# Two edits to a hybrid trunk kernel: where the first chunk products stand, and which engine multiplies row block 6 of the stick-breaking weights

## The chip, the cores and the metric

The kernel runs on one core of one Trainium2 chip. Its engines work side by side, each through its own list of instructions in a fixed order: TensorE (PE in the profile, PEld for its weight loads), VectorE (DVE), ScalarE (ACT), GpSimd (POOL) and SyncE (SP), which here mostly issues transfers. An instruction waits until what it needs is there, and everything behind it on the same engine waits with it. The metric is the time of one execution on the device in microseconds (us).

## The reference, cut to what matters

One layer on a sequence of 1024 tokens, model width 1024, float32. Three groups of heads mix the tokens, then comes a SwiGLU feed-forward part of hidden width 2816.

```python
h = rms_norm(x, attn_norm_g) @ w_in
r, k, v, wd, ad, gd = split(token_shift(h[..., :RW_COLS], mu))      # RWKV-7, 8 heads of 64
c_q, c_kv, k_rope, sb_q, sb_k, sb_v = split(h[..., RW_COLS:])       # latent, stick-breaking
# RWKV-7, per head and token:
S = S * w_t + (S @ a_t) b_t^T + v_t k_t^T        # a = -kk, b = kk * sigmoid(..), kk = normalised k
y_t = S @ r_t                                     # then group norm, bonus, gate
# stick-breaking, 4 heads of 64, s < t:
A[t, s] = sigmoid(z_ts) * prod_{s<j<t} (1 - sigmoid(z_tj));  y = A @ v
# latent attention, 4 heads: softmax over chunks up to the query's own
x = x + concat(y_rw, y_mla, y_sb) @ w_o
hn = rms_norm(x); x = x + (silu(hn @ w_gate) * (hn @ w_up)) @ w_down
```

## The kernel before, in words

A float32 product is made of three products of rounded parts (`mm3`, lines 207 to 209: high times high, high times low, low times high), so a projection of 128 columns against 512 tokens is 24 products. The weights of each are loaded by SP into `wr`, rounded into `wh` by ACT (line 185), and their rest `wl` comes from GpSimd (line 93, the helper that records every two-input operation).

**RWKV heads in pairs.** The eight heads go as four pairs `pr`, the 1024 tokens as two halves `hf`. `rw_block(pr, which)` projects k, r or v of one pair: two halves of 24 products each, then `shifted` (lines 288 to 298) takes them out of PSUM: ACT scales a half into SBUF (line 292), DVE adds the neighbour token's part (line 297). `between` is a tuple of functions that are called between the two halves and whose work is so written between them. `s1` makes the decays (u, ua, the scan `cs`, `Pe`, `iP`); `s2` makes the norm (ss, rs), kkn, and the factors `AR`, `BK` and `BD` of the chunk products, and `av`; `s3` makes the chunk products g (32 small products, masked by DVE into `gs`), and vt, bo and bkt, transposed copies that go out by DMA as `vs`, `av` and `bks`. `BD` has one buffer; PSUM has eight banks of 512 columns, shared in turn by projections, g, vt, bo, bkt, ss, u and ua.

**What sets the order.** The functions are written pair by pair so that the `s3` of one half stands between projections of the next. The program's builder then deals the instructions out to the engines by a cost model of its own, and each engine keeps that order. So an edit at one place can move rows at others.

**Stick-breaking.** For each of four heads and each row block i of 128 queries, `sb_weights` makes the scores z, two sigmoids on ACT (`st` and `w`), a running product `C` over the keys from the right (a scan on DVE, line 997, spans of up to 512 columns), and then w times C (line 93). `SB_POOL` (line 1110) lists the row blocks whose product w times C goes to GpSimd; the others go to DVE. The first entry of C is filled by GpSimd (line 985). `st`, `w` and `C` share a ring of five buffers. After it `av_tasks` transposes w on TensorE (wt, line 926), splits it (`wth` on ACT, `wtl` on DVE) and multiplies by v. In this stage the steps of the RWKV state chain (y, u, s) and the latent attention's rows are interleaved.

Of the kernel before, what the change touches and what calls it, by code (L numbers as in the profile page):

```python
# [59 lines left out]
def trunk_kernel(ctx: ExitStack, tc: tile.TileContext, a: dict, out: bass.AP):  # L60
# [17 lines left out]
    def bank(name, tag="b"):  # L78
        return psum["pool"].tile([P, HALF], F32, tag=tag, bufs=psum["tags"][tag], name=name)
# [12 lines left out]
    def tt(eng, o, x, y, op):  # L92
        eng.tensor_tensor(o, x, y, op=op)  # L93
# [21 lines left out]
    def vcol(r):  # L115
        return vec[:, r : r + 1]
# [109 lines left out]
    def inproj_cols(c0, name, between=()):  # L226

        if name in begun:
            return begun.pop(name)
        w = in_weights(c0, name)  # L230
        os_ = [in_half(w, 0, name)]
        for f in between:
            f()
        return os_ + [in_half(w, 1, name)]
# [53 lines left out]
    def shifted(dst, os_, cb):  # L288

        for hf in range(2):  # L290
            o, d_ = os_[hf], dst[hf]
            nc.scalar.activation(d_, o, AF.Copy, scale=omu[:, cb : cb + 1])
            if hf == 0:
                nc.vector.tensor_scalar_mul(car[:, cb : cb + 1], o[:, HALF - 1 : HALF], vcol(R_MU + cb))
            else:
                tt(nc.vector, d_[:, 0:1], d_[:, 0:1], car[:, cb : cb + 1], ALU.add)
            nc.vector.scalar_tensor_tensor(d_[:, 1:HALF], o[:, 0 : HALF - 1], vcol(R_MU + cb), d_[:, 1:HALF],
                                           op0=ALU.mult, op1=ALU.add)
# [50 lines left out]
    with tc.tile_pool(name="qa", bufs=1, reuse_waits="tile") as qa:  # L349
# [37 lines left out]
        def h2(name, tag, bufs=1):  # L387
            return qa.tile([P, HALF], F32, tag=tag, bufs=bufs, name=name)

        def ch8(ap):  # L390
            return ap.rearrange("p (c t) -> p c t", t=L)
# [24 lines left out]
        def rw_block(pr, which, between=()):  # L416

            t_ = [h2(f"{'KRV'[which]}{pr}{hf}", "KRV"[which], 3) for hf in range(2)]
            cb = (4 + pr, pr, 8 + pr)[which]
            shifted(t_, inproj_cols(cb * P, f"{'krv'[which]}{pr}", between), cb)  # L420
            KRV[pr][which] = t_
# [36 lines left out]
        def s2(pr, hf):  # L458
            n = f"{pr}_{hf}"
            sq, av, Pe, iP = tmp[n]  # L460
            k_, r_ = KRV[pr][0][hf], KRV[pr][1][hf]
            oss = bank(f"ss{n}")
            nc.tensor.matmul(oss, onesblk, sq, start=True, stop=True)
            rs_ = h2(f"rs{n}", "s1", 2)
            nc.scalar.activation(rs_, oss, AF.Ln, bias=EPS12)
            nc.scalar.activation(rs_, rs_, AF.Exp, scale=-0.5)
            kkn = h2(f"kkn{n}", "kkn")
            nc.vector.scalar_tensor_tensor(kkn, k_, vcol(R_KK + pr), rs_, op0=ALU.mult, op1=ALU.mult)
            AR = qa.tile([P, 8, 2, L], F32, tag="AR", bufs=2, name=f"AR{n}")
            BK = qa.tile([P, 8, 2, L], F32, tag="BK", bufs=2, name=f"BK{n}")  # L470
            nc.vector.scalar_tensor_tensor(AR[:, :, 0, :], ch8(kkn), -1.0, Pe[:, :, 0:64], op0=ALU.mult, op1=ALU.mult)
            tt(nc.gpsimd, AR[:, :, 1, :], ch8(r_), Pe[:, :, 1:65], ALU.mult)
            tt(nc.vector, kkn, kkn, av, ALU.mult)
            tt(nc.vector, BK[:, :, 0, :], ch8(kkn), ch8(iP), ALU.mult)
            nc.vector.tensor_scalar(av, av, vcol(R_KA + pr), oka[:, pr : pr + 1], op0=ALU.mult, op1=ALU.add)
            tt(nc.vector, av, av, k_, ALU.mult)
            tt(nc.vector, BK[:, :, 1, :], ch8(av), ch8(iP), ALU.mult)
            nc.vector.scalar_tensor_tensor(av, av, vcol(R_RK + pr), r_, op0=ALU.mult, op1=ALU.mult)

            BD = cp.tile([P, D], F32, tag="gB", name=f"BD{n}").rearrange("p (c t) -> p c t", c=8)  # L480
            dec = plt[:, pr, hf * 8 : hf * 8 + 8][:, :, None]
            tt(nc.gpsimd, BD[0:64], BK[0:64].rearrange("p c a t -> p c (a t)"), dec[0:64].to_broadcast([64, 8, 2 * L]), ALU.mult)
            for i in range(2):
                tt(nc.gpsimd, BD[64:128, :, (1 - i) * L : (2 - i) * L], BK[64:128, :, i], dec[64:128].to_broadcast([64, 8, L]), ALU.mult)
            for e in range(2):
                cs_, rows_ = slice(hf * 8, hf * 8 + 8), slice(e * 64, e * 64 + 64)
                lt_out(cs_, rows_, 2 * pr + e, AR[rows_].rearrange("p c a t -> p c (a t)"))
            tmp[n] = (AR, BK, BD, av)

        def s3(pr, hf):  # L490
            n = f"{pr}_{hf}"
            AR, BK, BD, rk = tmp[n]
            v_ = KRV[pr][2][hf]

            gs = [qa.tile([P, 8, P], F32, tag="gs", bufs=2, name=f"gs{n}_{e}") for e in range(2)]
            for q in range(2):
                ogs = [bank(f"g{n}_{e}{q}") for e in range(2)]
                for c in range(4):
                    for e, og in enumerate(ogs):
                        rows_ = slice(e * 64, e * 64 + 64)  # L500
                        nc.tensor.matmul(og[:, c * P : (c + 1) * P], BK[rows_, q * 4 + c].rearrange("p a t -> p (a t)"),
                                         AR[rows_, q * 4 + c].rearrange("p a t -> p (a t)"), start=True, stop=True)
                for e, og in enumerate(ogs):
                    tt(nc.vector, gs[e][:, q * 4 : q * 4 + 4], og.rearrange("p (c t) -> p c t", c=4),
                       gmask[:, None, :].to_broadcast([P, 4, P]), ALU.mult)
            cs_ = slice(hf * 8, hf * 8 + 8)
            for e in range(2):
                h = 2 * pr + e
                for b in range(2):
                    w = HB if b == 0 else L  # L510
                    nc.sync.dma_start(d_a[h, cs_, b, 0:w].rearrange("c s t -> s c t"), gs[e][0:w, :, b * HB : (b + 1) * HB])
                lt_out(cs_, R2[1 - e], h, gs[e][64:128])
                nc.sync.dma_start(d_rx[cs_, R2[e], h, :].rearrange("c s t -> s c t"), gs[e][0:64, :, 64:128])

            ov = bank(f"vt{n}")
            for j in range(4):
                nc.tensor.matmul(ov[:, j * P : (j + 1) * P], v_[:, j * P : (j + 1) * P], cent, start=True, stop=True)
            st = qa.tile([P, 4, P], F32, tag="st", bufs=2, name=f"vs{n}")
            nc.scalar.activation(st, ov.rearrange("p (c t) -> p c t", c=4), AF.Copy)
            for e in range(2):  # L520
                nc.sync.dma_start(d_v[e, hf * HALF : (hf + 1) * HALF, pr * L : (pr + 1) * L].rearrange("(j s) d -> s j d", s=P),
                                  st[:, :, e * L : (e + 1) * L])

            ob = bank(f"bo{n}")
            nc.tensor.matmul(ob, onesblk, rk, start=True, stop=True)
            tt(nc.vector, rk, ob, v_, ALU.mult)
            nc.sync.dma_start(d_bv[pr, :, hf * HALF : (hf + 1) * HALF], rk)
            for q in range(2):
                c0 = hf * 8 + q * 4
                ot = bank(f"bkt{n}_{q}")  # L530
                for c in range(4):
                    nc.tensor.transpose(ot[:, c * P : (c + 1) * P], BD[:, q * 4 + c], ident)
                st = qa.tile([P, 4, P], F32, tag="st", bufs=2, name=f"bks{n}_{q}")
                nc.scalar.activation(st, ot.rearrange("p (c t) -> p c t", c=4), AF.Copy)
                nc.sync.dma_start(d_bk[c0 : c0 + 4, :, pr * P : (pr + 1) * P].rearrange("c s d -> s c d"), st)
            if hf == 1:
                nc.sync.dma_start(d_pl[pr * P : (pr + 1) * P, :], plt[:, pr, :])
# [27 lines left out]
        for pr in range(4):  # L565
            if pr == 1:
                rotary()
            rw_block(pr, 0)
            if pr:
                rw_block(pr, 1, (lambda: s3(pr - 1, 0), lambda: s2(pr - 1, 1)))  # L570
                s1(pr, 0)
                rw_block(pr, 2)
                s3(pr - 1, 1)
            else:
                rw_block(pr, 1)
                rw_block(pr, 2, (lambda: s1(pr, 0),))
            s1(pr, 1)
            s2(pr, 0)
# [528 lines left out]

    FILL_INV, FILL_OUT, FILL_MG, FILL_END, FILL = 7.2, 12, 2, 10, 1.9
    LATE_PER_ATT = 1
    SB_POOL, MLA_POOL = (1, 3, 5), (1, 3, 5)  # L1110


    back["gen"] = background()
# [356 lines left out]
    with tc.tile_pool(name="q6", bufs=1, reuse_waits="tile") as q6:  # L1470
# [24 lines left out]
        for jj in range(NF // 2):  # L1495
# [15 lines left out]
            s1, s2, s3, s4 = up[0][1], up[1][1], up[0][0], up[1][0]  # L1511
# [153 lines left out]
```

## Time and profile before

| | us |
|---|---|
| median of three runs | 1431.05 |
| the three runs | 1431.5, 1431.05, 1429.12 |
| the profiled execution | 1427.67 |
| its span in the trace | 1426.0 |

The profiled execution is one run; its rows add up to its own time, which lies 3.38 us below the median of the three. The span is the stretch from the first to the last instruction. In the rows an engine's busy time, the idle time before an operation and the one that ended it stand together. PEclk is the share of full speed that the chip granted TensorE in a window.

### The profile page before, as it was taken

The numbers are of one execution on the slowest core, as the hardware profiler recorded it, in microseconds if no ns is written. First come the engines' busy times: TensorE is split into PE (matmuls) and PEld (weight loads), VectorE is DVE, ScalarE is ACT, GpSimd is POOL, SyncE is SP. The second block draws the span as 40 slices with busy tenths as digits, with TensorE's granted clock in tenths as the row PEclk, the third lists the DMA queues.
The fourth block names the chain that finished last, engine by engine and source line by source line (L and its number), as shares of the span: only waits on it lengthen the run. The fifth ranks groups of instructions, "written<-read, shape, count | busy, mean of one in ns | idle before, by whom it ended". The sixth has DMA issues, their size and how long they took to land.

```text
span 1426.0 us, 21466 instructions
## 1 busy us (share of the span) xinstructions
PE 1335.3 (94%) x7717; PEld 1101.4 (77%) x7717; DVE 924.3 (65%) x1316; ACT 656.7 (46%) x1308; POOL 686.9 (48%) x664
## 2 busy tenths in 40 slices
PE   7999999976898979998998899999999999999998
PEld 7877779855786757877886788888888888778786
DVE  5576777395237998676147955666565555797655
ACT  6755544233357868787225433333333333434342
POOL 2334343585333353225307766666666665544443
PEclk9999999997898999999999999999999999999999
DMA  7245667937779525624432433333223217842242
GB/s 222 64 93 127 148 145 172 229 97 185 210 211 258 182 85 174 187 73 141 153 119 76 132 105 111 111 104 111 89 103 111 82 67 288 317 166 100 82 140 74
DMA packets 224883, 201.28 MB, mean 141 GB/s; under 512 B 87133, under 2 KB 175498, under 8 KB 222858
## 3 DMA queue, kind: packets, MB, share of 16 engines
q1 hardware_dynamic: 202122, 170.29, 40.1%
q10 hardware_dynamic: 22656, 29.63, 6.9%
q8 instruction: 61, 1.00, 0.3%
q14 instruction: 44, 0.36, 0.1%
HBM read 131.95 MB, written 67.93 MB: 140 GB/s over the span
## 4 chain that ended last, share of the span: by engine, by line
PE 55%; DVE 9%; ACT 5%; issue 3%; POOL 2%; DMA 1%; ACTq 0%; DVEq 0%; SPq 0%; POOLq 0%
PE fd L208 4%; PE fd L209 4%; PE fd L207 4%; PE wo L209 2%; PE wo L208 2%; PE wo L207 2%; DVE C L997 2%; DVE wtl L93 1%; PE wt L926 1%; DVE xo L93 1%; ACT mw L1023 1%; DVE l_w L93 1%; PE y L1163 1%; PE P1up L207 1%; PE P3gate L208 1%
## 5 line engine op out<-in xcount | busy, mean ns | idle before, releaser
L93 POOL TENSOR_TENSOR l_h<-hr,h_h 128x512 fp32r<-128x512 f32 x77 | 106.5, 1384 | 107.3 <-ACT h_h L1323 102.3
L208 PE MATMUL fd<-l_w,h_h 128*128 128x512 f32 x308 | 120.0, 394 | 7.4 <-DVE l_w L93 7.2
L93 DVE TENSOR_TENSOR l_w<-wd,h_w 128x512 fp32r<-128x512 f32 x77 | 89.2, 1169 | 46.0 <-ACT h_w L1323 44.4
L209 PE MATMUL fd<-h_w,l_h 128*128 128x512 f32 x308 | 118.8, 391 | 0.0
L1323 ACT ACTIVATE h_h<-hr 128x512 fp32r<-128x512 f32 x77 | 48.7, 633 | 134.0 <-PE fd L208 89.1
L207 PE MATMUL fd<-h_w,h_h 128*128 128x512 f32 x308 | 84.3, 392 | 0.0
L93 POOL TENSOR_TENSOR l_ffn_w_up<-rffn_w_up,h_ffn_w_up 128x512 fp32r<-128x512 f32 x33 | 47.0, 1424 | 67.4 <-ACT h_ffn_w_up L1323 60.3
L208 PEld LDWEIGHTS fd<-l_w,h_h 128*128 128x128 f32 x308 | 58.1, 189 | 22.6 <-DVE l_w L93 10.6
L207 PEld LDWEIGHTS fd<-h_w,h_h 128*128 128x128 f32 x308 | 58.4, 190 | 12.3
L93 DVE TENSOR_TENSOR wtl<-wt,wth 128x512 fp32r<-128x512 f32 (+2 forms) x112 | 54.4, 492 | 20.5 <-ACT wth L931 16.0
L209 PEld LDWEIGHTS fd<-h_w,l_h 128*128 128x128 f32 x308 | 58.1, 189 | 11.9
L93 POOL TENSOR_TENSOR hid<-hid,up 128x512 f32<-128x512 f32 x44 | 62.6, 1423 | 9.3 <-DVE up L93 9.3
L93 POOL TENSOR_TENSOR BD<-BK,plt 64x512 f32<-64x512 f32 (+1 forms) x24 | 35.4, 1476 | 58.0 <-DVE BK L93 57.4
L93 POOL TENSOR_TENSOR l_ffn_w_gate<-rffn_w_gate,h_ffn_w_gate 128x512 fp32r<-128x512 f32 x33 | 48.0, 1456 | 20.6 <-ACT h_ffn_w_gate L1323 20.6
L931 ACT ACTIVATE wth<-wt 128x512 fp32r<-128x512 f32 (+2 forms) x112 | 48.4, 447 | 17.4 <-PE wt L926 6.0
L1504 ACT ACTIVATE hid<-hid 128x512 f32<-128x512 f32 x44 | 27.7, 632 | 60.6 <-DVE hid L93 60.6
L207 PE MATMUL wo<-woh,mix 128*128 128x512 f32 x128 | 50.7, 396 | 0.0
L209 PE MATMUL wo<-woh,mix 128*128 128x512 f32 x128 | 50.3, 393 | 0.0
L208 PE MATMUL wo<-wol,mix 128*128 128x512 f32 x128 | 50.3, 393 | 0.0
L1323 ACT ACTIVATE h_w<-wd 128x512 fp32r<-128x512 f32 x77 | 47.5, 617 | 1.3 <-PE P4up L208 0.9
L1323 ACT ACTIVATE h_ffn_w_gate<-rffn_w_gate 128x512 fp32r<-128x512 f32 x33 | 20.8, 631 | 56.9 <-PE P4up L208 21.5
L93 DVE TENSOR_TENSOR up<-hid,hid 128x512 f32<-128x512 f32 x22 | 28.1, 1318 | 19.6 <-POOL hid L93 19.6
(571 smaller groups left out, 4407.7 us busy)
## 6 DMA issues: line engine op xcount, KB each, us to landing
CT<-d_ch ACTq DMA_DIRECT2D x15, 1024.0 KB
hr<-d_h SPq DMA_DIRECT2D x14, 1024.0 KB
rffn_w_gate<-in_ffn_w_gate_dram SPq DMA_DIRECT2D x11, 1024.0 KB
rffn_w_up<-in_ffn_w_up_dram SPq DMA_DIRECT2D x11, 1024.0 KB
d_h<-up SPq DMA_DIRECT2D x44, 256.0 KB
d_h<-hid SPq DMA_DIRECT2D x33, 256.0 KB
wd<-in_ffn_w_down_dram SPq DMA_DIRECT2D x8, 1024.0 KB
hr<-d_h SPq DMA_DIRECT2D x7, 768.0 KB
```

What stands on the lines that cost most here:

```text
L93: eng.tensor_tensor(o, x, y, op=op)
L207: nc.tensor.matmul(o, lh, rh, start=first, stop=False)
L208: nc.tensor.matmul(o, lh, rl, start=False, stop=False)
L209: nc.tensor.matmul(o, ll, rh, start=False, stop=last)
L926: nc.tensor.transpose(o[:, (sb * 2 + i) * P : (sb * 2 + i + 1) * P], W[i][:, (2 * g + sb) * P : (2 * g + sb + 1) * P], ident)
L931: nc.scalar.activation(wh[:, lo:hi], o[:, lo:hi], AF.Copy)
L997: nc.vector.tensor_tensor_scan(C[:, k1 - 1 : last : -1], st[:, k1 - 1 : last : -1], zero_c.to_broadcast([P, k1 - k0]), 1.0 if k1 == n else ...
L1023: nc.scalar.activation(w[:, k0:k1], z, AF.Exp, scale=MLA_SCALE, bias=mx[:, 2:3], accum_out=mx[:, 4 + q : 5 + q])
L1163: nc.tensor.matmul(yo[:, ps[h]], Lt[:, h, :], S[:, ps[h]], start=h == 0, stop=True, skip_group_check=True)
L1323: nc.scalar.activation(hv, src, AF.Copy)
L1504: nc.scalar.activation(hid[f][hf], hid[f][hf], AF.Silu)
```

## The change

In the loop over the pairs, for pair 1 alone, `s3(0, 0)` is no longer called between the two halves of the r projection but behind both; `s2(0, 1)` stays between them. And `SB_POOL` gains row block 6, so its two products w times C, of 384 and 512 columns, go to GpSimd for each of the four heads.

```diff
--- before.py
+++ after.py
@@ -567,7 +567,12 @@
                 rotary()
             rw_block(pr, 0)
             if pr:
-                rw_block(pr, 1, (lambda: s3(pr - 1, 0), lambda: s2(pr - 1, 1)))
+                if pr == 1:
+
+                    rw_block(pr, 1, (lambda: s2(pr - 1, 1),))
+                    s3(pr - 1, 0)
+                else:
+                    rw_block(pr, 1, (lambda: s3(pr - 1, 0), lambda: s2(pr - 1, 1)))
                 s1(pr, 0)
                 rw_block(pr, 2)
                 s3(pr - 1, 1)
@@ -1107,7 +1112,7 @@
 
     FILL_INV, FILL_OUT, FILL_MG, FILL_END, FILL = 7.2, 12, 2, 10, 1.9
     LATE_PER_ATT = 1
-    SB_POOL, MLA_POOL = (1, 3, 5), (1, 3, 5)
+    SB_POOL, MLA_POOL = (1, 3, 5, 6), (1, 3, 5)
 
 
     back["gen"] = background()
```

On TensorE, around the second half of pair 1's r projection (ip_r; g, vt, bo and bkt belong to the first half of pair 0, ss to its second half), the difference reads, with the repeated products left out:

```order
-L501 MATMUL g_0_00_974<-AR_0_817,BK_0_818 128x128
...
-L517 MATMUL vt_0_1007<-cent,V_700 128x128 x4
-L525 MATMUL bo_0_1016<-av_0_745,onesblk 128x512
...
-L532 MATMUL bkt_0_1_1028<-ident,BD_0_827 128x128 x4
...
+L463 MATMUL ss_1_972<-sq_1_787,onesblk 128x512
+L207 MATMUL ip_r_996<-xT_110,wh_r_942 128x512
...
+L501 MATMUL g_0_00_1029<-AR_0_817,BK_0_818 128x128
...
+L517 MATMUL vt_0_1062<-cent,V_700 128x128 x4
+L525 MATMUL bo_0_1071<-av_0_745,onesblk 128x512
...
+L532 MATMUL bkt_0_1_1083<-ident,BD_0_827 128x128 x4
 L410 MATMUL u_0_1093<-wa_584,lo_582 128x512
```

The second half of r and the ss before it now come first, and the products from g to bkt stand behind them, right ahead of u.

On DVE, in the same place (gs and av_0 belong to the first half of pair 0, the kkn_1 to BK_1 chain to its second half, R_940 empties the second half of r):

```order
L93 TENSOR_TENSOR gs_0_0_972<-g_0_00_974,gmask 128x512
L93 TENSOR_TENSOR gs_0_1_973<-g_0_10_975,gmask 128x512
L93 TENSOR_TENSOR gs_0_0_972<-g_0_01_986,gmask 128x512
L93 TENSOR_TENSOR gs_0_1_973<-g_0_11_987,gmask 128x512
L93 TENSOR_TENSOR av_0_745<-bo_0_1016,V_700 128x512
L468 SCALAR_TENSOR_TENSOR kkn_1_1041<-K_629,vec,rs_1_1038 128x512
L471 SCALAR_TENSOR_TENSOR AR_1_1043<-kkn_1_1041,Pe_1_805 128x8x64
L93 TENSOR_TENSOR kkn_1_1041<-kkn_1_1041,av_1_799 128x512
```

and now:

```order
L475 TENSOR_SCALAR av_1_799<-av_1_799,vec,oka 128x512
L93 TENSOR_TENSOR av_1_799<-av_1_799,K_629 128x512
L93 TENSOR_TENSOR BK_1_980<-av_1_799,iP_1_807 128x8x64
L93 TENSOR_TENSOR R_940<-R_940,car 128x1
L297 SCALAR_TENSOR_TENSOR R_940<-ip_r_996,vec,R_940 128x511
L93 TENSOR_TENSOR gs_0_0_1027<-g_0_00_1029,gmask 128x512
L93 TENSOR_TENSOR gs_0_1_1028<-g_0_10_1030,gmask 128x512
L478 SCALAR_TENSOR_TENSOR av_1_799<-av_1_799,vec,R_637 128x512
L93 TENSOR_TENSOR gs_0_0_1027<-g_0_01_1041,gmask 128x512
L93 TENSOR_TENSOR gs_0_1_1028<-g_0_11_1042,gmask 128x512
```

The four gs and the bo product moved behind R_940, two of them also behind the product av_1 with R_637.

On GpSimd, in the first stick-breaking head at row blocks 5 to 7 (w is the weights, C the running product):

```order
L93 TENSOR_TENSOR gupl<-gup,guph 128x512
L93 TENSOR_TENSOR w_5_4433<-w_5_4433,C_5_4434 128x256
L93 TENSOR_TENSOR w_5_4433<-w_5_4433,C_5_4434 128x512
L93 TENSOR_TENSOR w_6_4475<-w_6_4475,C_6_4476 128x384
L93 TENSOR_TENSOR w_6_4475<-w_6_4475,C_6_4476 128x512
L990 MEMSET C_7_4538 128x1
L990 MEMSET C_0_4602 128x1
```

The two products of row block 6 stand behind those of row block 5 and ahead of the fill of C for row block 7.

## Rows read from the trace of the kernel before

**Rows 1.** The page's first part: busy time, share of the span and instructions of each engine.

```profile
PE 1335.3 (94%) x7717; PEld 1101.4 (77%) x7717; DVE 924.3 (65%) x1316; ACT 656.7 (46%) x1308; POOL 686.9 (48%) x664
```

**Rows 2.** Windows around the change: stretch, length, busy times, PEclk, DMA share, GB/s.

```profile
71.00:107.00 36.00, 33.23 (x159) 26.47 (x157) 26.55 (x29) 19.18 (x29) 13.65 (x9) 0.91 0.42 93
107.00:143.00 36.00, 36.00 (x208) 28.63 (x207) 25.30 (x31) 17.96 (x29) 16.05 (x12) 1.00 0.56 127
```

**Rows 3.** The timeline of PE: start, duration, operation; idle before and its releaser.

```profile
86.62 0.39 PE L209 MATMUL ip_r<-xT,wl_r 128*128 128x512 f32 x1
89.78 3.79 PE L501 MATMUL g<-AR,BK 64*128 64x128 f32 x32 [2.77 <-DVE BK L93]
...
97.31 1.02 PE L463 MATMUL ss<-sq,onesblk 128*128 128x512 f32 x2
97.77 0.79 PE L207 MATMUL ip_r<-xT,wh_r 128*128 128x512 f32 x1
...
103.67 0.40 PE L410 MATMUL u<-wa,lo 128*128 128x512 f32 x1
...
105.28 0.50 PE L207 MATMUL ip_v<-xT,wh_v 128*128 128x512 f32 x1
```

**Rows 4.** The timeline of PE, the same products of the next half.

```profile
116.38 2.06 PE L501 MATMUL g<-AR,BK 64*128 64x128 f32 x32
...
121.14 0.49 PE L410 MATMUL u<-wa,lo 128*128 128x512 f32 x1
```

**Rows 5.** The timeline of DVE around the gs products.

```profile
94.52 2.47 DVE L93 TENSOR_TENSOR gs<-g,gmask 128x512 f32<-128x512 f32 x4
...
100.29 0.75 DVE L468 SCALAR_TENSOR_TENSOR kkn<-K,vec,rs 128x512 f32<-128x512 f32 x1 [2.70 <-ACT rs L466]
...
103.71 1.42 DVE L93 TENSOR_TENSOR av<-av,K 128x512 f32<-128x512 f32 x1
105.16 2.76 DVE L93 TENSOR_TENSOR BK<-av,iP 128x512 f32<-128x512 f32 x1
...
107.92 0.74 DVE L297 SCALAR_TENSOR_TENSOR R<-ip_r,vec,R 128x511 f32<-128x511 f32 x1
108.58 1.87 DVE L478 SCALAR_TENSOR_TENSOR av<-av,vec,R 128x512 f32<-128x512 f32 x1
```

**Rows 6.** The timeline of POOL beside them.

```profile
103.39 1.19 POOL L93 TENSOR_TENSOR BD<-BK,plt 64x512 f32<-64x512 f32 x1 [10.25 <-DVE BK L93]
104.88 2.50 POOL L93 TENSOR_TENSOR wl_k<-wr_k,wh_k 128x1024 fp32r<-128x1024 f32 x1 [0.30 <-DMA d_ch<-gs]
```

**Rows 7.** The timeline of ACT beside them.

```profile
103.69 1.06 ACT L185 ACTIVATE wh_k<-wr_k 128x1024 fp32r<-128x1024 f32 x1 [3.43 <-issue]
...
106.15 0.60 ACT L534 ACTIVATE bks<-bkt 128x512 f32<-128x512 f32 x1 [0.83 <-DMA d_v<-vs]
```

**Rows 8.** Windows of the stick-breaking stage, columns as above.

```profile
463.00:499.00 36.00, 33.22 (x351) 28.14 (x347) 34.07 (x57) 30.52 (x79) 13.40 (x25) 1.00 0.59 180
499.00:535.00 36.00, 27.50 (x161) 20.87 (x161) 34.43 (x63) 24.32 (x61) 18.05 (x23) 0.91 0.28 85
```

**Rows 9.** Groups of instructions by line and shape in the stage: count, busy, mean ns.

```profile
L997 DVE TENSOR_TENSOR_SCAN C<-st,C,bias_n 128x512 f32<-128x512 f32 x16 | 24.0, 1498 | 2.7 <-ACT st L993 2.3
...
L93 DVE TENSOR_TENSOR w<-w,C 128x512 f32<-128x512 f32 x16 | 12.6, 784 | 0.5 <-ACT w L994 0.2
...
L93 POOL TENSOR_TENSOR w<-w,C 128x512 f32<-128x512 f32 x8 | 9.9, 1239 | 8.4 <-DVE C L997 4.5 <-ACT yn L1207 3.9
...
L93 DVE TENSOR_TENSOR w<-w,C 128x384 f32<-128x384 f32 x8 | 4.4, 549 | 0.4
```

**Rows 10.** The chain that ended last, in the stage: start, duration, work.

```profile
478.53 1.50 DVE w L93 x2
...
511.12 1.28 DVE C L997
...
521.96 1.81 DVE C L997
```


## The prediction

> **What bounds the kernel now.** I read the busy slices first, then the windows, then the two engines that answer each other in the two places of the change, and the chain of waits last. TensorE is busy for 1335.3 of 1426.0 us [rows 1]: a gain must either close one of its idle gaps or shorten a stage in which another engine sets the pace. The first part of the change touches a gap, the second such a stage.
>
> The first place is the window from 71 to 107 us, where TensorE is busy 33.23 of 36 us and its granted clock is 0.91, while in the next 36 us it is busy 36.00 at 1.00 [rows 2]. The missing 2.77 us are one gap: the first half of the r projection issues its last product at 86.62, and the g products wait until 89.78 for DVE's BK [rows 3]. Behind that gap TensorE was slower: these g products take 3.79 us, the same 32 of the next half 2.06 [rows 3, 4]. That is what a clock between the levels of 1.2 and 2.4 GHz does in the mean; the granted clock says that it was the chip's and not a wait. From g to the start of ss it is 7.53 us (89.78 to 97.31) [rows 3], in the next half from g to u 4.76 us (116.38 to 121.14) [rows 4]: 2.77 us for the clock. Since TensorE is full from 107 to 143 us, what is won or lost before is carried on.
>
> The second place is the stick-breaking stage. From 463 to 535 us DVE is busy 34.07 and 34.43 of 36 us, TensorE 33.22 and 27.50 [rows 8]. DVE sets the pace there, and the chain of waits goes through its scans and, at 478.53, through row 6's pair of products [rows 10].
>
> **The r projection in one piece.** Removed is the order "g, vt, bo, bkt, ss, second half of r"; now it is "ss, second half of r, g, vt, bo, bkt". The work is the same. The second half's 24 products run from 97.77 to 103.67, 5.90 us [rows 3], and ss has long had its input; so they fill the gap: from 86.87 (86.62 and a spacing of about a quarter us) ss and r reach 93.2. BK is there by 89.8, g runs at once, and at the short durations of rows 4 the last bkt but one ends at about 97.5. Were this all, u would start at about 98 and not at 103.67: 5.5 us, the gap and the clock together.
>
> It is not all. TensorE's eight PSUM banks go round, and the last bkt group takes the bank that the second half of r filled. In the order of DVE the R that empties it stands behind the seven operations from kkn to BK of the other half, and the gs products stand behind R. Before, kkn starts at 100.29 and R ends at 108.66 (107.92 and 0.74): 8.37 us [rows 5]. Now kkn need not wait for rs and starts where the gs products stood, at 94.52 [rows 5]. In those 8.37 us GpSimd's BD stretched av to 1.42 and wl_k stretched BK to 2.76 (kkn, also with two inputs from SBUF, takes 0.75 with GpSimd idle) [rows 5, 6]. BD has one buffer and now waits for the last bkt, so av's 0.67 (1.42 less 0.75) falls away. wl_k stays: wh_k, which it subtracts, waits for the last r product, as at 103.69 before [rows 7], and now comes at 93.5, so wl_k's 2.50 us lie in the same chain. R then ends at 94.52 + 8.37 - 0.67 = 102.2. Behind it: two gs at 0.62 (2.47 over 4), the product av (1.87, beside BD as before), one gs: 102.2 + 1.24 + 1.87 + 0.62 = 105.9, and there the v projection can start, whose bank that gs empties. Before it starts at 105.28 [rows 3]: 0.6 us later, estimated. If wl_k came too early or too late to hold anything, 2.01 (BK) and 1.12 (av) go, and it starts 2.5 us earlier: that is the other end.
>
> So what the order gains at the gap is given back behind it: TensorE waits from 97.5 to 102.2 for R, a gap of 4.7 us in place of 2.77. The clock is the next term. After the gap of 2.77 us the slow stretch cost 2.77 us. The new gap is longer; if the clock falls again, bkt, u and ua run slow while they wait for DVE anyway, and the v projection pays for the rest. I take half, 1.4 us, the ends being 0 and 2.8. What is queued behind the waiting bkt is u, ua and the v projection, and through the vs and bks copies ACT; the gs transfers leave SP some 8 us later, but what they feed is read much later, and the V copies that now stand behind a landing have some 10 us until the next g products [rows 4]. I cost them at nothing; if that cover is gone it costs one transfer's wait of the kind that held bks for 0.83 us [rows 7]. First part: +0.6 + 1.4 = **+2.0 us**, ends -2.5 and +3.4 + 0.8 = +4.2.
>
> **Row 6 on GpSimd.** DVE loses four times one product of 384 and one of 512 columns: 4 x (0.549 + 0.784) = 5.3 us [rows 9]. GpSimd gets them. A product of 512 takes it 1.239 [rows 9]; one of 384 isn't shown, and by its columns it is 0.93. So 4 x 2.17 = 8.7 us on an engine that is busy 13.40 and 18.05 of 36 us [rows 8]. There is room, but not for free. DVE's scans of 512 columns with a carried start take 1.28 alone (511.12) and 1.81 at 521.96; the mean over 16 is 1.498 [rows 9, 10]. At a GpSimd share of 44% (31.45 of 72 us) an operation of DVE lost 17%, so at a full share some 39%, and the 8.7 us cost DVE about 3.4 us, estimated. Net on DVE: -5.3 + 3.4 = -1.9 us. The ends: none of it collides, -5.3; all of it does, 8.7 - 5.3 = +3.4.
>
> The Trainium skill (SBUF — State Buffer, "Who interferes with whom") says that a DVE instruction with two inputs in SBUF and a GpSimd instruction that reads SBUF exclude each other, the one that comes second waiting in full, and advises to put on GpSimd only what is off the critical path. The stretched av, BK and scan above are such pairs and agree. By that rule in its strict form the end of +3.4 us would be the sum; the operations of DVE that read PSUM, such as wtl and gs, are free of it.
>
> Row 6 is also ready later: 2.17 in place of 1.33 us a head. Behind it on GpSimd stands the fill of C for row 7 in the first head, on which row 7's scan waits, and in the chain of before row 6's products stood at least once; in all four heads 4 x 0.84 would be 3.4 us, of which I take a small part, 0.4, since DVE has scans and wtl of other rows in between. The order of heads, chain steps and rows is dealt out anew from here to the end of the stage; I have no row for what that brings and count it at zero. Second part: **-1.5 us**.
>
> **The sum** is +2.0 - 1.5 = +0.5 us on the profiled execution's 1427.67 us. The median shown is 1431.05, so 3.38 us above it: 1428.2 + 3.4 = **1431.6 us**. What this kernel's measurement can tell from no change is about 0.2%, 2.9 us.
>
> **The rivals.**
> 1. *Nearly nothing, my forecast:* the gap moves behind the g products and the stage gains little; own range 1429 to 1434. Chance 0.37.
> 2. *Faster:* wl_k misses the chain (-2.5), and the clock stays up behind the new gap; the gap was due to DVE, so TensorE keeps most of what it fills. With -1.9 to -5.3 from the stage it is -4.4 to -7.8, about 1425. For it: the DVE work from kkn on starts 5.8 us earlier than before (94.52 and not 100.29). Against it: wh_k is also earlier, by 10 us. Chance 0.32.
> 3. *Slower, at the bank:* the last bkt waits for R, the clock falls and the v projection pays in full: +0.6 + 2.8, with 0.8 for a late landing +4.2. If the stage gives nothing, 1435. It decides when R ends later than about 101.6 (then the v projection can't start earlier than before) and the granted clock between 71 and 107 us is no higher than 0.91. For it: the only gap here was followed by a slow stretch. Chance 0.21.
> 4. *Slower, on GpSimd:* row 6 collides in full, +3.4, and row 7's scan waits for it in two heads, 2 x 0.84 = +1.7: with the first part's +2.0 about 1438. For it: the chain goes through DVE's scans, the very ones that are held up. Against it: a good part of DVE's work there reads PSUM. Chance 0.10.
>
> Below about 1425 I leave one in ten, above 1438 the same: the range is 1425 to 1438. Faster by over 0.2% is case 2, 0.32; within 0.2% is case 1, 0.37; slower are cases 3 and 4, 0.31.
>
> **What would show it.** In the changed kernel's profile: the second half of r follows the first without a gap; g takes about 2.1 and not 3.8 us; a new gap of about 4.7 us stands ahead of the last bkt, released by DVE's R; wl_k lies beside DVE's kkn-to-BK chain; the v projection starts at 105 to 107 us. If it starts before 103.5, my account of the bank is wrong. In the stage, DVE's busy time from 420 to 550 us falls by 1 to 3 us although 5.3 us of products left it, and the mean of the 512-column scans rises above 1.5 us. If DVE falls by 5 us, the collisions were over-priced; if the stage's length changes by over 4 us either way, it is the new order that decided and not these eight products.

## The result, and where the time went

The changed kernel takes 1437.76 us in the median of 16 runs, the kernel before 1430.47 (16 runs beside them): ratio 1.0058, interval 1.0047 to 1.0069. By the ratio it is slower by 8 us; the forecast was no change. The profiled execution took 1434.5 us (span 1432.8), 6.8 us over that of before. Both lie some 3 us below the medians of their kernels, and single profiles of one order differ by several microseconds in places that matter here, so the trace alone doesn't say where the loss arises.

At its own place the first part went as worked out. TensorE in the changed kernel (start, duration, operation, idle before and its releaser):

```profile
86.72 1.02 PE L463 MATMUL ss<-sq,onesblk 128*128 128x512 f32 x2
87.18 0.80 PE L207 MATMUL ip_r<-xT,wh_r 128*128 128x512 f32 x1
...
93.16 2.06 PE L501 MATMUL g<-AR,BK 64*128 64x128 f32 x32
...
97.00 0.60 PE L532 MATMUL bkt<-ident,BD 128*128 128x128 f32 x4
102.15 1.02 PE L532 MATMUL bkt<-ident,BD 128*128 128x128 f32 x4 [4.55 <-DVE R L297]
102.82 0.77 PE L410 MATMUL u<-wa,lo 128*128 128x512 f32 x1
...
105.69 0.79 PE L207 MATMUL ip_v<-xT,wh_v 128*128 128x512 f32 x1
...
108.42 0.63 PE L207 MATMUL ip_v<-xT,wh_v 128*128 128x512 f32 x1
...
118.38 2.06 PE L501 MATMUL g<-AR,BK 64*128 64x128 f32 x32
```

Against [rows 3, 4] the old gap ahead of g is closed and g takes 2.06 in place of 3.79 us. A gap of 4.55 us stands ahead of the last bkt, released by DVE's R. Behind it the products are slow again (0.63 a product until 108.8, 0.39 or 0.40 after), and the g products of the next half come at 118.38 in place of 116.38: 2.00 us late. The windows (PE busy, then DVE, ACT, POOL behind PEld, then the granted clock) show the slow stretch moved into the second one, 0.97 for the 1.00 of [rows 2]:

```profile
71.00:107.00 36.00, 31.45 (x153) 24.15 (x153) 28.51 (x33) 20.13 (x30) 16.31 (x11) 0.93 0.30 74
107.00:143.00 36.00, 36.00 (x186) 28.25 (x187) 18.76 (x23) 17.48 (x27) 13.91 (x10) 0.97 0.66 143
```

What the clock does behind the old gap, however, differs from one execution to the next. [rows 2, 3] come from a single one. Eight of the kernels below have the order of before up to the stick-breaking stage, and the same gap of 2.8 us ahead of g. In three of their profiles the granted clock from 71 to 107 us is 1.00 and g takes 2.06 us; in five it is 0.95 and g takes 2.89 to 3.49 us; in the profile of before it is 0.91 and g takes 3.79. Here are g and the g of the next half with FILL at 1.8, then with the 384 columns of row block 6 on GpSimd:

```profile
89.64 2.06 PE L501 MATMUL g<-AR,BK 64*128 64x128 f32 x32 [2.77 <-DVE BK L93]
...
114.28 2.06 PE L501 MATMUL g<-AR,BK 64*128 64x128 f32 x32
```

```profile
89.69 3.49 PE L501 MATMUL g<-AR,BK 64*128 64x128 f32 x32 [2.77 <-DVE BK L93]
...
114.91 2.06 PE L501 MATMUL g<-AR,BK 64*128 64x128 f32 x32
```

In the eight the next g products come at 114.3 to 115.2 us. The profile of before, with 116.38, is the slowest of nine at this place, and against the other eight the changed kernel is 3.2 to 4.1 us late there and not 2.0.

DVE in the same place, to be held against [rows 5]:

```profile
94.48 2.70 DVE L468 SCALAR_TENSOR_TENSOR kkn<-K,vec,rs 128x512 f32<-128x512 f32 x1
...
100.58 0.69 DVE L93 TENSOR_TENSOR BK<-av,iP 128x512 f32<-128x512 f32 x1
...
101.26 0.74 DVE L297 SCALAR_TENSOR_TENSOR R<-ip_r,vec,R 128x511 f32<-128x511 f32 x1
101.92 1.28 DVE L93 TENSOR_TENSOR gs<-g,gmask 128x512 f32<-128x512 f32 x2
103.11 0.74 DVE L478 SCALAR_TENSOR_TENSOR av<-av,vec,R 128x512 f32<-128x512 f32 x1
103.77 1.28 DVE L93 TENSOR_TENSOR gs<-g,gmask 128x512 f32<-128x512 f32 x2
```

and GpSimd beside it:

```profile
94.28 2.35 POOL L93 TENSOR_TENSOR wl_k<-wr_k,wh_k 128x1024 fp32r<-128x1024 f32 x1 [1.19 <-ACT wh_k L185]
103.25 5.39 POOL L93 TENSOR_TENSOR BD<-BK,plt 64x1024 f32<-64x1024 f32 x3 [6.62 <-DVE gs L93]
```

wl_k now lies under kkn, which takes 2.70 in place of 0.75 us; that is all that the chain loses to it, and R ends at 102.0. BD came after R and stretched none of the rows shown; av, 0.74 here, had begun at 103.11, before it.

Against the profile of before, the lag of 2.0 us holds until the last chunk products at 250 us. At 273.13 the sk projection waits 4.99 us for DVE's stlsq, which it did not before, and the lag is 7.2 us; at the latent up-projection ukv most of that is given back, because the kernel before waited there itself. First the changed kernel:

```profile
273.13 0.80 PE L207 MATMUL ip_sk<-xT,wh_sk 128*128 128x512 f32 x1 [4.99 <-DVE stlsq L93]
...
315.99 0.50 PE L207 MATMUL ukv<-ukvh,ct0ckv 128*128 128x512 f32 x1 [1.13 <-DVE ct1cq L743]
```

and the kernel before at the same product:

```profile
312.89 0.50 PE L207 MATMUL ukv<-ukvh,ct0ckv 128*128 128x512 f32 x1 [2.91 <-DVE ct1cq L738]
```

So the lag is 3.1 us at 316, and it stays near 3.4 until the stick-breaking stage. The wait at sk costs nothing that can be seen: in the five kernels with r in one piece, sk and ukv together wait 5.0 to 7.1 us, and in the nine with the old order ukv alone waits 5.0 to 7.9. The nine begin the stage at 414.3 to 417.4 us, 415.6 in the mean, so the 3.4 us are what was lost at 116 us against the typical execution.

The length of the stage, with the latent attention behind it, is read from two groups, the first score product z and the first product of w_o (count: shortest, median and longest duration, first and last start). In the changed kernel:

```profile
L994 PE MATMUL z<-sqk,sqk x48: 221/401/776, 419.0 to 540.5; 128*128 128x512 f32 x24, 128*128 128x128 f32 x8, 128*128 128x256 f32 x8, 128*128 128x384 f32 x8
...
L207 PE MATMUL wo<-woh,mix x128: 389/393/477, 677.7 to 770.8; 128*128 128x512 f32 x128
```

and in the kernel before:

```profile
L989 PE MATMUL z<-sqk,sqk x48: 221/428/775, 415.5 to 534.6; 128*128 128x512 f32 x24, 128*128 128x128 f32 x8, 128*128 128x256 f32 x8, 128*128 128x384 f32 x8
...
L207 PE MATMUL wo<-woh,mix x128: 389/393/477, 671.5 to 764.7; 128*128 128x512 f32 x128
```

258.7 in place of 256.0 us: 2.7 longer, lag 6.2. Two single profiles don't show that the order made the stage longer: three kernels below that have the very order of before in the stage take 255.2, 257.7 and 261.0 us for it in their profiles (the pair-1 edit alone, R emptied first, the chain taken away). The lag is 8.3 us when the first up products of the feed-forward part start, and 6.8 at the end. The extra two microseconds lie between 785 and 800 us, where TensorE waits for the rounded sums in both kernels. The granted clock from 785 to 805 us is 0.84 here and 0.99 before; the changed kernel's window first, then that of before:

```profile
785.00:805.00 20.00, 13.71 (x43) 9.83 (x44) 19.59 (x13) 8.26 (x9) 10.37 (x6) 0.84 0.17 54
```

```profile
785.00:805.00 20.00, 16.27 (x69) 12.50 (x68) 19.48 (x17) 9.53 (x15) 10.40 (x7) 0.99 0.50 157
```

Order and work are the same there. Of the twelve other kernels below, eleven have 0.83 to 0.91 and one 1.00, so the profiled execution of before did well there, and these two microseconds can't be counted as a price of the change.

The stage's own rows, beside [rows 9]:

```profile
L1002 DVE TENSOR_TENSOR_SCAN C<-st,C,bias_n 128x512 f32<-128x512 f32 x16 | 25.0, 1561 | 3.4 <-ACT st L998 2.8
...
L93 POOL TENSOR_TENSOR w<-w,C 128x512 f32<-128x512 f32 x12 | 13.7, 1144 | 10.5 <-DVE C L1002 9.2 <-DVE gnr L1223 1.2
...
L93 DVE TENSOR_TENSOR w<-w,C 128x512 f32<-128x512 f32 x12 | 8.5, 727 | 0.3 <-ACT w L999 0.2
...
L93 POOL TENSOR_TENSOR w<-w,C 128x384 f32<-128x384 f32 x4 | 3.5, 866 | 2.0 <-DVE C L1002 1.0 <-DVE gnv L1237 1.0
```

By the means of the groups row block 6 costs GpSimd 4 x (0.866 + 1.144) = 8.0 us, near the forecast, and the carried scans of DVE rise from 1498 to 1561 ns. What DVE gained is read from the stage's own windows, from the first z to the first w_o (PE busy, PEld, DVE, ACT, POOL): before, the pair-1 edit alone, row block 6 alone, the changed kernel.

```profile
415.50:671.50 256.00, 224.53 (x1918) 186.12 (x1917) 204.17 (x449) 197.31 (x493) 96.17 (x128) 0.94 0.53 159
```

```profile
418.70:673.90 255.20, 224.13 (x1918) 185.66 (x1917) 204.82 (x449) 197.58 (x493) 96.27 (x128) 0.94 0.53 159
```

```profile
416.80:676.00 259.20, 226.87 (x1918) 187.62 (x1917) 204.07 (x441) 197.27 (x493) 103.18 (x136) 0.92 0.53 157
```

```profile
419.00:677.70 258.70, 227.69 (x1919) 188.13 (x1918) 204.55 (x441) 197.04 (x493) 103.10 (x136) 0.91 0.53 157
```

Row block 6 takes 0.1 us off DVE's busy time without the pair-1 edit (204.17 to 204.07) and 0.3 with it (204.82 to 204.55), although 5.3 us of products left DVE. What stayed on DVE got longer by some 5 us, where the forecast had 3.4.

### The profile page after: what moved, and what is told of

It is laid out like the page before. It is cut to its first block, busy times and chain, and to the rows that moved or that the text cites. A ratio compares the mean times of both kernels' runs of the same rounds, so it can differ in the third digit from the quotient of the medians.

```text
span 1432.8 us, 21463 instructions
## 1 busy us (share of the span) xinstructions
PE 1338.5 (93%) x7717; PEld 1102.1 (77%) x7717; DVE 921.6 (64%) x1308; ACT 657.5 (46%) x1308; POOL 695.6 (49%) x672
## 4 chain that ended last, share of the span: by engine, by line
PE 47%; DVE 3%; issue 1%; POOL 1%; ACT 0%; DVEq 0%; ACTq 0%; POOLq 0%
PE fd L208 4%; PE fd L209 4%; PE fd L207 4%; PE wo L209 2%; PE wo L208 2%; PE wo L207 2%; DVE l_w L93 1%; PE P7gate L209 1%; PE P7gate L208 1%; PE P7gate L207 1%; PE P6gate L208 1%; PE P3gate L208 1%; PE P3gate L207 1%; PE P3gate L209 1%; PE P3up L209 1%
## 5 line engine op out<-in xcount | busy, mean ns | idle before, releaser
L93 DVE TENSOR_TENSOR wd<-wd,wd 128x512 f32<-128x512 f32 x44 | 39.7, 933 | 0.6
## 6 DMA issues: line engine op xcount, KB each, us to landing
d_h<-up SPq DMA_DIRECT2D x44, 256.0 KB
d_h<-hid SPq DMA_DIRECT2D x33, 256.0 KB
```

## The experiments

Two theories stood: (1) the two parts add, each with its own price, the first through R; (2) the newly dealt order of the stage decides. The rivals within the second part were the amount of GpSimd work, the lateness of row 6, and the order. Each ratio is to the kernel before on the same chip, from five rounds. The parts can be cut cleanly: with the pair-1 edit alone the stage's order is that of before, with row 6 alone it is that of the changed kernel, row for row.

**The pair-1 edit alone.**

```diff
-    SB_POOL, MLA_POOL = (1, 3, 5, 6), (1, 3, 5)
+    SB_POOL, MLA_POOL = (1, 3, 5), (1, 3, 5)
```

> Only the pair-1 edit: the second half of r ahead of the g products; SB_POOL stays (1, 3, 5). Theory 1 (the two parts add; the bank wait behind R and the slow stretch put the chunk products of pair 0's second half 2.0 us later, and that is carried on): g of that half starts 2.0 us later than before, the time is 2 to 3.5 us over the kernel before, ratio 1.0014 to 1.0025. Theory 2 (the stick-breaking stage's new order decides, and the lag of the first part is taken up by the waits at 300 to 345 us): ratio 1.000 +- 0.0007.

Ratio 1.0028 (1.0014 to 1.0043), 4 us slower. The trace has the same gap and the next g products 2.34 us after those of the profile of before:

```profile
102.15 0.76 PE L532 MATMUL bkt<-ident,BD 128*128 128x128 f32 x4 [4.54 <-DVE R L297]
...
118.72 2.06 PE L501 MATMUL g<-AR,BK 64*128 64x128 f32 x32
```

Against the eight other profiles with the old order there they are 3.6 to 4.4 us late, which is what the ratio says. The part loses by itself; theory 2's version, that the lag is taken up, falls.

**Row block 6 alone**, the same line of the kernel before changed the other way.

> Only row block 6 on GpSimd, the r projection as before. Theory 1 (the parts add): +3 to +5 us, ratio 1.002 to 1.0035, so that both together make the 1.0058 measured. Theory 2 (the stage's new order decides alone): +7 to +8 us, ratio 1.005 to 1.0056. My prediction's term for this part was -1.5 us, ratio 0.999.

Ratio 1.0017 (0.9999 to 1.0034): about 2.4 us, on the side of a loss but not clear of none. The 1.5 us of gain that were forecast, 0.9990, lie outside, and so does theory 2. 0.0028 and 0.0017 make 0.0045, within reach of the 0.0058 measured (0.0047 to 0.0069), so adding parts agree with the runs; by difference the second costs 0.0030, some 4 us.

**The bank wait and the DVE chain taken away.**

```diff
-                    rw_block(pr, 1, (lambda: s2(pr - 1, 1),))
-                    s3(pr - 1, 0)
+                    rw_block(pr, 1)
+                    s3(pr - 1, 0)
+                    s2(pr - 1, 1)
```

> The pair-1 edit with the bank wait taken away: the two halves of r stand together, R of the second half is emptied by DVE right behind R of the first, then come the g products, and the norm and the kkn-to-BK chain of the other half behind them. SB_POOL as before. Theory 1 (the first part lost because the last bkt waits for R behind the kkn-to-BK chain): no gap ahead of the last bkt, the v projection starts near 99.5 us instead of 105.28, g of the next half some 5 us earlier, granted clock 1.00 from 71 to 107 us, time 3 to 5.5 us below the kernel before, ratio 0.996 to 0.998. Rival (what is won before 120 us is taken up by later waits on transfers and DVE): the v projection is as early, but the ratio is 0.999 to 1.000.

Ratio 0.9981 (0.9963 to 0.9999). TensorE from 92 to 111 us, and its window (busy 36.00 of 36, granted clock 1.00):

```profile
92.22 2.06 PE L501 MATMUL g<-AR,BK 64*128 64x128 f32 x32
...
97.61 0.76 PE L410 MATMUL u<-wa,lo 128*128 128x512 f32 x1
...
99.60 0.50 PE L207 MATMUL ip_v<-xT,wh_v 128*128 128x512 f32 x1
...
110.74 2.06 PE L501 MATMUL g<-AR,BK 64*128 64x128 f32 x32
```

```profile
71.00:107.00 36.00, 36.00 (x182) 28.40 (x181) 27.82 (x31) 21.16 (x31) 15.49 (x11) 1.00 0.42 91
```

Gap and slow stretch are both gone and the next g products are 5.64 us earlier than in the profile of before (110.74 for 116.38), 3.5 to 4.4 us earlier than in the eight others. With the wait for R and the chain ahead of it both taken away, a loss of 0.0028 becomes a gain of 0.0019, and the two intervals don't meet: that the first part lost through them is so shown. The stage is entered at 411.6 us, 4 us ahead of the mean of the nine, and 2.7 us arrive by the ratio; with its interval (0.1 to 5.3 us) this doesn't show that anything was lost on the way.

**R emptied first, the chain still written ahead of the g products.**

```diff
-                    rw_block(pr, 1, (lambda: s2(pr - 1, 1),))
-                    s3(pr - 1, 0)
+                    rw_block(pr, 1)
+                    s2(pr - 1, 1)
+                    s3(pr - 1, 0)
```

> The pair-1 edit with R of the second half emptied by DVE right behind R of the first, so that the last bkt's bank is free early; but the kkn-to-BK chain of the other half still stands ahead of the gs products on DVE, as in the change. SB_POOL as before. If the bank held by R is the cause by itself: no gap at the last bkt and a gain as in the run with the chain behind the gs products, ratio 0.997 to 0.999. If it is the chain on DVE ahead of everything that frees a bank: the wait moves one row down to u, whose bank the first gs empties at about 102.5 us, and the ratio is 1.001 to 1.003 as with the pair-1 edit alone.

Ratio 1.0018 (1.0002 to 1.0034), but not for the reason expected. The builder put the gs products in between the chain's first operations, and nothing waits there: the v projection starts at 99.45 us. A wait comes one half later, and the clock falls behind it:

```profile
114.40 0.60 PE L532 MATMUL bkt<-ident,BD 128*128 128x128 f32 x4
117.54 0.63 PE L532 MATMUL bkt<-ident,BD 128*128 128x128 f32 x4 [2.54 <-DVE V L297]
```

```profile
107.00:143.00 36.00, 33.46 (x190) 25.43 (x190) 22.62 (x30) 16.64 (x26) 14.27 (x11) 0.95 0.62 142
```

It is the same kind of wait with V in place of R: a bank that is emptied late by DVE, here because ACT's copy of V stands behind a bks copy that waits 2.99 us for a transfer, and behind four more operations of ACT. The next g products but one, at 138.75 us, are 1.5 us ahead of the profile of before and level with the eight others (138.2 to 139.1): what was won is gone there. So the wait for R alone was not all; the chain has to move too. Where the remaining loss of about 2.6 us (0.3 to 4.9) comes from I did not settle; the stage's order is that of before.

**Other rows on GpSimd.** Row block 6 in place of 5, `SB_POOL = (1, 3, 6)`:

> Row blocks 1, 3 and 6 on GpSimd in place of 1, 3 and 5; the r projection as before. GpSimd's and DVE's sums in the stage stay within 0.7 us of before, but the order of the stage is dealt out anew. If the loss of the second part is the amount of GpSimd work (its collisions with DVE): +-1 us of the kernel before, ratio 0.9993 to 1.0007. If it is that row block 6 itself is late (row 7's fill and buffer stand behind it): as slow as row 6 added, ratio 1.002 to 1.004. If the new order by itself decides, anything within 0.996 to 1.005, and the stage's length follows no sum of busy times.

Ratio 0.9985 (0.9971 to 0.9999). Row block 4 in place of 6, `SB_POOL = (1, 3, 4, 5)`:

> Row block 4 (128 and 512 columns a head) added to GpSimd in place of row block 6; the r projection as before. If the second part lost by the amount of GpSimd work that collides with DVE: also slower, ratio 1.001 to 1.002. If it lost because row block 6 stands just ahead of row block 7 at a head's end: not slower, ratio 0.9985 to 1.000. If the newly dealt order decides, no relation, 0.997 to 1.003.

Ratio 1.0043 (1.0027 to 1.0059). Only the 384 columns of row block 6:

```diff
-            tt(nc.gpsimd if i in SB_POOL else nc.vector, ...
+            tt(nc.gpsimd if i in SB_POOL or (i == 6 and k0) else nc.vector, ...
```

> Only the product of 384 columns of row block 6 goes to GpSimd (3.5 us in all in place of 8.3); that of 512 columns stays on DVE. If collisions by amount decide: a loss of about 0.4 of the full edit's 1.0017, ratio 1.0007. If the order decides: anywhere from 0.997 to 1.003.

Ratio 1.0029 (1.0012 to 1.0045). Less than half of the work moved, and no less was lost; so the loss does not follow the amount. Nor does it follow DVE's busy time. This kernel's stage,

```profile
415.90:674.20 258.30, 225.88 (x1919) 186.94 (x1918) 199.78 (x445) 197.10 (x493) 101.13 (x132) 0.93 0.53 161
```

has 4.4 us less of DVE than that of before (199.78 for 204.17), and the kernel is slower. Row 6 in place of row 5 gains a little, so row 6 is not bad in itself. Row 7's fill of C on DVE, with row 6 on GpSimd:

```diff
-        nc.gpsimd.memset(C[:, n : n + 1], 1.0)
+        (nc.vector if i == 7 else nc.gpsimd).memset(C[:, n : n + 1], 1.0)
```

> Row block 6 on GpSimd as in the change, r projection as before, and the fill of C for row block 7 moved to DVE, so that row 7's scan no longer stands behind row 6's products on GpSimd. If that wait was the second part's loss: the loss is gone, ratio 0.999 to 1.000. If not: as slow as without it, 1.001 to 1.0025.

Ratio 1.0022 (1.0006 to 1.0038): that wait was not it either.

**The order by itself.** With every instruction on its engine, only FILL, the planner's share of other work between state steps, goes from 1.9 to 1.8 and to 2.0.

> Order alone: row blocks 1, 3, 5 on GpSimd and the r projection as before, every instruction on the engine it had; only the planner's share of other work between the steps of the state chain (FILL) is 1.8 in place of 1.9, which deals out the stage anew. If the order by itself is worth as much as the second part of the change: a ratio outside 0.9990 to 1.0010, either way. If not: within it.

Ratio 0.9980 (0.9966 to 0.9994).

> Order alone, the other way: FILL is 2.0 in place of 1.9, engines as before. Same reading: outside 0.9990 to 1.0010, either way, if the order by itself is worth as much as the second part; within it if not.

Ratio 1.0066 (1.0040 to 1.0091). The two groups that bound the stage, and its window, with FILL 2.0:

```profile
L989 PE MATMUL z<-sqk,sqk x48: 220/459/794, 416.3 to 541.7; 128*128 128x512 f32 x24, 128*128 128x128 f32 x8, 128*128 128x256 f32 x8, 128*128 128x384 f32 x8
...
L207 PE MATMUL wo<-woh,mix x128: 389/393/477, 683.1 to 776.3; 128*128 128x512 f32 x128
```

```profile
416.30:683.10 266.80, 234.38 (x1918) 193.96 (x1917) 206.67 (x449) 196.79 (x493) 96.14 (x128) 0.90 0.52 153
```

266.8 us, with the same work, for 255.2 to 261.0 in the four profiles that have the order of before. A slower TensorE goes along with it: the mean granted clock of these six runs is 0.959 to 0.968, that of the runs of before beside them 0.966 to 0.972. And with row block 6 on GpSimd at FILL 2.0:

> Row block 6 on GpSimd, the r projection as before, and the stage dealt out with FILL at 2.0. If row 6's work on GpSimd costs by itself, it is slower than the run with FILL 2.0 alone by 0.0015 to 0.003. If the order decides, the difference to it has any size and sign.

Ratio 0.9985 (0.9964 to 1.0006), a profiled stage of 259.8 us:

```profile
L989 PE MATMUL z<-sqk,sqk x48: 220/408/792, 417.4 to 541.4; 128*128 128x512 f32 x24, 128*128 128x128 f32 x8, 128*128 128x256 f32 x8, 128*128 128x384 f32 x8
...
L207 PE MATMUL wo<-woh,mix x128: 387/393/477, 677.2 to 770.3; 128*128 128x512 f32 x128
```

```profile
417.40:677.20 259.80, 230.22 (x1919) 190.15 (x1918) 199.05 (x441) 196.01 (x493) 105.69 (x136) 0.91 0.53 155
```

At FILL 1.9 the row costs 0.0017, not clear of nothing; at 2.0 it gains 0.0081 (1.0066 to 0.9985), well clear. DVE's busy time in the stage falls by 7.6 us here (206.67 to 199.05), for 0.1 to 0.3 at FILL 1.9. So what the same eight products are worth, and how much they collide, depends on the order they are dealt into. How much of the second part's loss in the changed kernel is collision and how much is order stays open: no run adds row block 6 on GpSimd at FILL 1.9 in another order of the rest. Which pair of rows in an order makes it long was not found.

**Both gains together**: r in one piece with the chain behind g, and `SB_POOL = (1, 3, 6)`.

> Both gains together: the r projection in one piece with R emptied first and the kkn-to-BK chain behind the g products, and row blocks 1, 3 and 6 on GpSimd in place of 1, 3 and 5. If the two parts add: ratio 0.9981 + 0.9985 - 1 = 0.9966, some 5 us below the kernel before. If the stage's length depends on when it is entered, or both gains were the spread of this measurement: 0.998 to 1.000.

Ratio 0.9966 (0.9952 to 0.9980), 1424.78 us in the median, 1430.0 before: 5 us faster than the kernel before, as the sum of the two, and 0.9 per cent below the changed kernel.

## Why the prediction was wrong

- *r runs ahead of g, g at full clock:* right. 2.06 us, r at 87.18 with no gap.
- *The last bkt waits for R behind the DVE chain:* right in place and size. R ends at 102.0 (102.2 forecast), the gap is 4.55 us (4.7), the v projection starts at 105.69 (105.9). Of the chain's stretching only the place was wrong: wl_k met kkn and not BK. That the v start fits so well is in part luck. The forecast let it wait for the last gs; that ended at 105.05, and TensorE came to v without a gap behind u and ua, which ran slow (0.77 and 0.79 us each, 0.40 to 0.50 before). With the pair-1 edit alone v does wait for gs, 0.48 us, and starts at 106.09.
- *First part, +2.0 us:* the mechanism was right, the size too small. The next g products are 2.00 us behind those of the profile of before, but alone the part costs 4 us (2.0 to 6.2 by the interval). The term that fails is "the slow stretch cost 2.77 us": it was read from one execution and taken as what the gap of before costs. In eight others the same gap cost less or nothing in clock, and the next g products came 1.2 to 2.1 us earlier; held against those, the part's price is already 3.2 to 4.1 us at its own place. The later copies and landings, put at nothing, show no price of their own.
- *Second part, -1.5 us:* this is the step that failed in sign, and its two terms failed separately. DVE was to gain 1.9 us net, 5.3 less 3.4 for collisions; in the stage it gained 0.1 to 0.3, so what stayed on DVE got some 5 us longer and not 3.4. (In the window that the forecast named, 420 to 550 us, DVE falls by 3.4 us, but only because work has moved out of it into the rest of the stage.) And "I have no row for what that brings and count it at zero" put at nothing a term that is as large as any: order alone moves this kernel by -0.2 to +0.7 per cent. Behind both stands the same reading, that the stage's time follows DVE's sum. DVE is busy for 95% of 72 us of the stage but for 80% of its 256, and with 4.4 us less of DVE the 384-column kernel is slower. What the forecast gave as the sign of a new order, a stage changed by over 4 us, did not appear; the runs with FILL show the order, not the changed kernel's trace.
- *The rivals.* None came true as written. By its time, 1435 us, the third is near, slower at the bank with the stage giving nothing; it had 0.21. R did end later than 101.6, but the granted clock from 71 to 107 us was 0.93 and not 0.91 or less, and v did not pay in full at its place. Of rival 4's two mechanisms, row 7's wait for its fill is refuted by the fill on DVE; that row 6 collides fits DVE's busy time, but the 384-column run shows that the loss does not follow the amount. That 1437.76 us still lies inside the stated range, 0.2 us below its end, is luck of a wide range and no sign that a case was understood.
- *The exclusion of DVE and GpSimd* that the Trainium skill describes (SBUF — State Buffer, "Who interferes with whom") is there in the trace, kkn's 2.70 for 0.75 us under wl_k. Its strict form, +3.4 us on DVE by amount, is more than the trace shows: DVE's busy time in the stage did not rise.

## What to carry to other kernels

When a block of products is moved to fill a gap, follow the buffers that it fills to the instruction that empties them, in that engine's order: here the gap moved to the next product that needed the bank, and moving the emptying and the chain ahead of it along with it turned a loss of 4 us into a gain of about 3. Price a slow stretch of the clock from several executions, since the same gap had a long one, a short one or none. Where a builder deals out a whole stage anew after a small edit, the new order has its own price: measure two or three other orders of the same work before an edit's gain or loss is put down to the work it moves. And combine edits only after each has been measured alone.

## What the runs showed that I had not expected

A change of one planning number, without moving one instruction to another engine, costs 1.0066, as much as the whole change (1.0058); the two intervals overlap. And the place that the first part was to mend looked worse in the one profile that the forecast was made from than in any of eight others with the same order there: 116.38 us against 114.3 to 115.2 at the next g products.
